# A two-layer three-branch decoder trunk: gating constants made early, row scaling on ScalarE, one more pair of columns as seven products, and a shorter last sum of squares

## The chip, the cores and the metric

One core of a Trainium2 chip runs the whole computation in one launch. Its engines are named as in the profile: PE (TensorE, matrix products into PSUM), DVE (VectorE), ACT (ScalarE), POOL (GpSimd) and SP (SyncE, which here only issues DMAs). The metric is the device time of one execution in microseconds (us). Most executions of a kernel agree within 0.3%.

## The reference, cut to what matters

Each of two layers normalizes x (512 tokens, 1024 channels, float32), projects it on 8704 columns, mixes tokens in three branches and adds a gated, projected merge to x. A last RMSNorm follows.

```
def hybrid_layer(x, ...):
    h = rmsnorm(x, norm_g)
    aq, ak, av, az, buv, bz, cq, ck, cv, cz, gl = split_cols(h @ w_in)
    # A: differential attention, then RMSNorm over each head's 128 outputs
    oa = rmsnorm(diff_attention(qa, ka, va, lam), subln_g) * (1 - lam_init)
    ya = oa * silu(az)
    # B: causal spatial gating in chunks of 128 tokens
    u, vb = split(gelu(buv));  vb = layernorm(vb, sgu_ln_g, sgu_ln_b)
    w_causal = sgu_w * tril(ones(128, 128))
    mixed = einsum('gts,bnsgc->bntgc', w_causal, vb) + sgu_b
    yb = u * mixed * silu(bz)
    # C: three dilated window attentions, mixed by their softmax sums
    yc = oc * silu(cz)
    pb = [ya @ w_branch[0], yb @ w_branch[1], yc @ w_branch[2]]
    merged = sum(sigmoid(gl[n]) * pb[n] for n in range(3))
    return x + merged @ w_out
out = rmsnorm(layer_2(layer_1(x)), final_g)
```

## The kernel before, in words

The state is kept transposed, channels on partitions and tokens in the free dimension. Every projection is done in float32 by three products of rounded parts (`mm3`, L408 to 411: high by high, low by high, high by low). A weight half of 128x512 numbers, a slot, is rounded by ScalarE into its high part (L170), and the remainder is the low part (L171), on VectorE or, for every fifth slot after the first 32, on POOL (`LOMOD`, `FIRST_G`). Two raw buffers of 512 KB are filled from SP's queue (`load`), and up to six slots are made ahead (`NSLOT`).

A pair of 128-column blocks is projected in one of two ways. Those listed in `EIGHT` take 24 products of 512 columns for each block (`proj_T`, L417). All others take seven products of quarters in place of eight (`seven`, L503), with 256 columns in each product: seven slots (L176 to 203) of which four are made from sums of raw quarters by POOL, VectorE, POOL, POOL (L192 to 195), and combinations of the products by ScalarE (L531, L535), VectorE and POOL (`add`, L528). The sums of quarters lie in tiles of the tag `pr`, two buffers, which attention's probabilities use too (L862).

`plan` (L50) lists the items of a layer in order. First come the gating values `vb`, the values of A (with the normalized x made beside them), the values of C (with the mixed quarters made beside them, `mix`, L596) and one pair. Then attention A runs over four heads in three steps each, and the remaining pairs are pulled in as fill between its products; the two second-gate pairs `bz2` (columns of bz, multiplied into u by POOL at L653) are the second last projection in attention A and the last in attention C. Attention C follows in the same way, and then the gating step `sgu`, in turn with the sigmoid gates `gl2` and the branch projections `pb`, and last the output projection `out`.

`i_sgu` (L657) loads the bias row and the 128x512 matrix for the layer from ScalarE's queue, after the newest weight instructions (`behind_weights`), lets POOL clear the upper triangle (L666), sums the matrix over its partitions by a product with ones (L671) and makes `add` from it, bias and the layernorm's shift, four VectorE instructions on 128x128 (L675). After that it does four groups: four products (L685), two VectorE instructions (L690, L695), one split.

In attention A, after a head's third step, VectorE multiplies the head's 128x512 outputs in PSUM by four row factors (`scaled`, L943; the factors come from POOL at L941), and `finish` transposes the result and applies the gate. In the last layer the output blocks 4 to 7 are done for the left 256 tokens and then for the right 256; `square` (L278) sums squares over blocks, `rms_sum` (L380) sums over partitions by small products with ones, and `final` (L824) normalizes and stores.

Each engine works through its own list in order. The lists are written by a planner that takes the program's order and priorities and its own simulated times, so an edit can move instructions that it does not touch.

Of the kernel before, what the change touches and what calls it, by code (L numbers as in the profile page):

```python
# [10 lines left out]
F32 = mybir.dt.float32  # L11
# [32 lines left out]


EIGHT = {("pp", br, i) for br in (BR_A, BR_C) for i in range(6) if (br, i) != (BR_C, 5)}
EIGHT |= {("bz2", 0), ("bz2", 2), ("gl2", BR_B, 0)}


def plan():  # L50
# [50 lines left out]
def hybrid_kernel(ctx: ExitStack, tc, xT, posr, wpack, tabs, cvec, pvec, rvec, lamv, sguw, outT):  # L101
# [149 lines left out]
    class X:  # L251


        def __init__(self, first=False):
            self.first = first
            self.h = att.tile([P, KC, S], F32R, tag="vs", name="xuh")
            self.l = []
            self.f = []
            self.ss = t2k("ob", name="ssum")

        def raw(self, kc):
            if kc % 2 == 0:
# [15 lines left out]
        def square(self, kc, c=slice(0, S), part=False):  # L278
            xf = self.f[kc // 2][:, kc % 2, c]
            if kc == 0:  # L280
                A.activation(out=self.ss[:, c], in_=xf, func=AF.Square)
            else:
                sq = t2k("t1", name="sq")
                A.activation(out=sq[:, c], in_=xf, func=AF.Square)
                if part and kc == KC - 1:
                    self.sq = sq
                    return
                (V if kc == KC - 1 or self.first or c.start else G).tensor_tensor(out=self.ss[:, c], in0=self.ss[:, c], in1=sq[:, c], op=ALU.add)

# [90 lines left out]
    def rms_sum(sqs):  # L380

        n = sqs[0].shape[-1] // P
        ps = ps_s()[:, 0, :]
        for b in range(n):
            for i, sq in enumerate(sqs):
                T.matmul(
                    ps[:, b : b + 1], lhsT=sq[:, b * P : (b + 1) * P], rhs=ones[:, 0:1], start=i == 0,
                    stop=i == len(sqs) - 1,
                )
        ro = sm.tile([P, 4], F32, tag="ro", name="ro")[:, :n]  # L390
        V.tensor_scalar(out=ro, in0=ps[:, :n], scalar1=1.0 / D, scalar2=EPS, op0=ALU.mult, op1=ALU.add)
        rp = sm.tile([P, 4], F32, tag="rp", bufs=2, name="rp")[:, :n]
        G.tensor_tensor(out=rp, in0=ro, in1=mhalf[:, :n], op=ALU.pow)
        return rp
# [153 lines left out]
    def layer(l, xu, parts):  # L548
# [47 lines left out]
        def mix(kc):  # L596
            with behind_weights():
                if kc == 0:
                    split_x(KC - 1)
                    norm["mix"] = mixes(xu.f)  # L600
                next(norm["mix"])
                if kc == KC - 1:
                    next(norm["mix"])
                    if l == 0:
                        lambdas()

        def pair(it, use, bank=ps_pj):

# [47 lines left out]

        def i_sgu():  # L657
            vb, uz = sgu["vb"], sgu["uz"]
            sgw = [att.tile([P, S], F32, tag="kl", bufs=2, name="sgw") for _ in range(2)]
            with behind_weights():  # L660
                nc.scalar.dma_start(out=sgw[0], in_=rvec[l : l + 1, :].partition_broadcast(P))
                nc.scalar.dma_start(out=sgw[1], in_=sguw[l])
            t = att.tile([P, 2, 4, S], F32R, tag="vs", name="yB")
            yhl[BR_B] = [[t[:, 0, 0:2], t[:, 0, 2:4]], [t[:, 1, 0:2], t[:, 1, 2:4]]]
            wc = sgw[1].rearrange("p (g t) -> p g t", g=4)
            G.affine_select(  # L666
                out=wc, in_=wc, pattern=[[0, 4], [1, P]], base=0, channel_multiplier=-1, compare_op=ALU.is_ge,
                fill=0.0,
            )
            pw = ps_s()[:, 0, :]  # L670
            T.matmul(pw, lhsT=ones, rhs=sgw[1], start=True, stop=True)  # L671
            add = t2k("t1", name="add")
            for g in range(4):
                gs = slice(g * P, (g + 1) * P)
                V.scalar_tensor_tensor(  # L675
                    out=add[:, gs], in0=pw[:, gs], scalar=ln[:, l, 1, g : g + 1], in1=sgw[0][:, gs], op0=ALU.mult,
                    op1=ALU.add,
                )
            yield 0.9
            for g in range(4):  # L680
                if g % 2 == 0:
                    pms = ps_s()
                pm = pms[:, g % 2, :]
                for tb in range(4):
                    T.matmul(  # L685
                        pm[:, tb * P : (tb + 1) * P], lhsT=vb[:, tb, g * P : (g + 1) * P],
                        rhs=wc[:, g, :], start=True, stop=True,
                    )
                ob = t2k("ob")
                V.scalar_tensor_tensor(  # L690
                    out=ob.rearrange("p (n t) -> p n t", n=4), in0=pm.rearrange("p (n t) -> p n t", n=4),
                    scalar=ln[:, l, 0, g : g + 1],
                    in1=add[:, g * P : (g + 1) * P].unsqueeze(1).to_broadcast([P, 4, P]), op0=ALU.mult, op1=ALU.add,
                )
                V.scalar_tensor_tensor(  # L695
                    out=ob, in0=ob, scalar=0.25, in1=uz[g // 2][:, g % 2, :], op0=ALU.mult, op1=ALU.mult
                )
                split(yhl[BR_B][0][g // 2][:, g % 2, :], yhl[BR_B][1][g // 2][:, g % 2, :], ob)
                yield 0.9

        def i_val(br):
            if br == BR_A:
# [12 lines left out]
            for tb in range(4):  # L715
                p8 = banks[tb].rearrange("p (h e) -> p h e", h=8)
                r, o = norm["rst"][:, tb : tb + 1], v[:, tb]
                A.activation(out=o[:, :, 0:64], in_=p8, func=AF.Copy, scale=r)
                V.scalar_tensor_tensor(
                    out=o[:, :, 64:128], in0=p8, scalar=r, in1=o[:, :, 0:64].bitcast(F32), op0=ALU.mult,  # L720
                    op1=ALU.subtract,
                )

        def i_pp(br, i):
            def use(n, ps, own):
# [97 lines left out]

        def final(c):  # L824
            x_ = xn[0]
            bc = rms_spread(rms_sum([x_.ss[:, c], x_.sq[:, c]]))
            for e in range(KC):
                xf = x_.f[e // 2][:, e % 2, c]
                V.scalar_tensor_tensor(out=xf, in0=xf, scalar=fg[:, e : e + 1], in1=bc, op0=ALU.mult, op1=ALU.mult)
                (nc.sync, nc.scalar)[e % 2].dma_start(out=outT[e, :, c], in_=xf)  # L830
# [70 lines left out]
        def attention_a(fill):  # L901
# [4 lines left out]
            for n in range(13):  # L906
# [10 lines left out]
                if prev is not None:  # L917
# [20 lines left out]
                    if 3 in prs:  # L938
# [3 lines left out]

                        def scaled(po_=po_, r0_=so_):  # L943
                            on = t2k("ob", name="on").rearrange("p (i e) -> p i e", i=4)
                            V.tensor_tensor(
                                out=on, in0=po_, in1=r0_.unsqueeze(2).to_broadcast([P, 4, P]), op=ALU.mult
                            )
                            return on

                        def finish(h=h):  # L950
# [197 lines left out]
```

## Time and profile before

| | |
|---|---|
| median of 3 executions | 1116.62 us (1115.82 to 1116.85) |
| the profiled execution | 1117.34 us, span 1115.6 us |
| PE busy | 1087.3 us, 97% of the span |
| DVE busy | 823.6 us, 74% |
| ACT busy | 598.9 us, 54% |
| POOL busy | 471.4 us, 42% |
| HBM read | 100.58 MB, 94 GB/s with what is written |

The span is what the profiler saw between the first and the last instruction. Products on PE are pipelined, and their ends are modelled; the distance of two starts is what one of them takes of PE's time. An idle engine only costs where something on the way to the end waits for it.

### The profile page before, as it was taken

To read this page: it belongs to the slowest core of one execution; us is meant where nothing else is said; L and a number is where in the kernel's file an instruction comes from. 1 tells how busy PE (TensorE), PEld (TensorE's weight loads), DVE (VectorE), ACT (ScalarE), POOL (GpSimd) and SP (SyncE) were. 2 spreads that over 40 slices of the span, in tenths; PEclk is the share of its full clock that TensorE was granted. 3 is DMA by queue.
4 is the path that set the end of the run, shared out by engine and by line. 5 is a ranking of instruction groups with operands and counts; after the bars stand their busy time and mean duration, and the time that the engine had idled before them with its cause. 6 is when DMAs were issued, how large, how long until landed. Compare 5 with 4: busy or idle time off the path is not lost.

```text
span 1115.6 us, 17803 instructions
## 1 busy us (share of the span) xinstructions
PE 1087.3 (97%) x6444; PEld 939.6 (84%) x6444; DVE 823.6 (74%) x1519; ACT 598.9 (54%) x1281; POOL 471.4 (42%) x419
## 2 busy tenths in 40 slices
PE   8999999999999999999999999999999999999996
PEld 6787878878778999998888888887888889999886
DVE  6678869877969877774436779787788877787544
ACT  6554747486774444453435456565778534444430
POOL 4004443434534676644211343534342536667420
PEclk9999999999999999999999999999999999999998
DMA  5431313220312233244523313122111313333433
GB/s 194 135 103 58 95 58 96 95 76 1 114 58 87 87 112 102 92 148 152 188 83 103 98 38 114 57 76 76 58 58 57 112 59 101 107 97 103 142 110 99
DMA packets 35064, 105.97 MB, mean 95 GB/s; under 512 B 4704, under 2 KB 7776, under 8 KB 34976
## 3 DMA queue, kind: packets, MB, share of 16 engines
q1 hardware_dynamic: 29936, 98.50, 27.6%
q10 hardware_dynamic: 5040, 6.34, 1.8%
q8 instruction: 51, 0.84, 0.3%
q14 instruction: 37, 0.30, 0.1%
HBM read 100.58 MB, written 4.24 MB: 94 GB/s over the span
## 4 chain that ended last, share of the span: by engine, by line
PE 85%; DVE 5%; DMA 3%; issue 2%; ACT 2%; POOL 1%; POOLq 0%; DVEq 0%; SPq 0%; ACTq 0%
PE ps_pj L409 15%; PE ps_pj L411 14%; PE ps_pj L410 14%; PE ps_to L409 8%; PE ps_to L411 8%; PE ps_to L410 8%; PE ps_s L858 3%; DMA raw<-in_wpack 2%; PE ps_to L898 2%; PE ps_to L434 2%; PE ps_to L436 2%; PE ps_to L435 2%; DVE wlo L171 1%; PE ps_to L929 1%; PE ps_to L1004 1%
## 5 line engine op out<-in xcount | busy, mean ns | idle before, releaser
L170 ACT ACTIVATE whi<-raw 128x512 fp32r<-128x512 f32 x316 | 195.0, 627 | 246.3 <-DMA raw<-in_wpack 74.2
L171 DVE TENSOR_TENSOR wlo<-raw,whi 128x512 fp32r<-128x512 f32 x261 | 223.0, 862 | 99.2 <-ACT whi L170 91.1
L409 PE MATMUL ps_pj<-xh,whi 128*128 128x512 f32 (+1 forms) x544 | 207.9, 382 | 1.0 <-DVE z L462 1.0
L411 PE MATMUL ps_pj<-xh,wlo 128*128 128x512 f32 (+1 forms) x544 | 204.5, 376 | 0.0
L410 PE MATMUL ps_pj<-xl,whi 128*128 128x512 f32 (+1 forms) x544 | 204.0, 375 | 0.0
L171 POOL TENSOR_TENSOR wlo<-raw,whi 128x512 fp32r<-128x512 f32 x55 | 78.8, 1433 | 169.6 <-ACT whi L170 158.2
L409 PEld LDWEIGHTS ps_pj<-xh,whi 128*128 128x128 f32 x544 | 102.6, 189 | 20.0 <-issue 1.6
L411 PEld LDWEIGHTS ps_pj<-xh,wlo 128*128 128x128 f32 x544 | 102.5, 188 | 18.2 <-issue 0.9
L410 PEld LDWEIGHTS ps_pj<-xl,whi 128*128 128x128 f32 x544 | 102.7, 189 | 17.6 <-issue 1.8
L452 POOL TENSOR_TENSOR rsh<-rsh,sinr 128x512 f32<-128x512 f32 x32 | 42.3, 1322 | 132.8 <-DVE rsh L450 121.3
L171 DVE TENSOR_TENSOR wlo<-t,whi 128x512 fp32r<-128x512 f32 x88 | 81.2, 940 | 16.2 <-ACT whi L170 16.0
L411 PE MATMUL ps_to<-mh,wlo 128*128 128x256 f32 x320 | 90.5, 284 | 0.5 <-DVE wlo L171 0.4
L409 PE MATMUL ps_to<-mh,whi 128*128 128x256 f32 x320 | 90.8, 284 | 0.2 <-ACT ea L531 0.2
L410 PE MATMUL ps_to<-ml,whi 128*128 128x256 f32 x320 | 90.4, 283 | 0.0
L874 ACT ACTIVATE pr<-pr,nm 128x128 f32<-128x128 f32 (+3 forms) x128 | 70.6, 553 | 36.4 <-DVE nm L870 36.1
L170 ACT ACTIVATE whi<-t 128x512 fp32r<-128x512 f32 x112 | 65.8, 624 | 42.0 <-DVE t L193 23.4
L409 PE MATMUL ps_to<-xh,whi 128*128 128x256 f32 x240 | 68.5, 285 | 2.6 <-DVE zs L528 2.5
L411 PE MATMUL ps_to<-xh,wlo 128*128 128x256 f32 x240 | 68.4, 286 | 0.7 <-DVE wlo L171 0.7
L410 PE MATMUL ps_to<-xl,whi 128*128 128x256 f32 x240 | 68.2, 284 | 0.0
L870 DVE CUSTOM_DVE_ANT_0 pr<-ps_s,tab 128x128 f32<-128x128 f32 (+3 forms) x128 | 56.2, 483 | 11.8 <-PE ps_s L858 8.3
L409 PEld LDWEIGHTS ps_to<-mh,whi 128*128 128x128 f32 x320 | 61.4, 192 | 1.0 <-ACT ea L531 0.4
L411 PEld LDWEIGHTS ps_to<-mh,wlo 128*128 128x128 f32 x320 | 61.3, 192 | 1.2 <-DVE wlo L171 0.9
(238 smaller groups left out, 2844.9 us busy)
## 6 DMA issues: line engine op xcount, KB each, us to landing
raw<-in_wpack SPq DMA_DIRECT2D x174, 512.0 KB
xf<-in_xT SPq DMA_DIRECT2D x8, 256.0 KB
xr<-in_xT ACTq DMA_DIRECT2D x8, 256.0 KB
x1d<-xf SPq DMA_DIRECT2D x8, 256.0 KB
raw<-in_wpack SPq DMA_DIRECT2D x4, 256.0 KB
xr<-x1d ACTq DMA_DIRECT2D x4, 256.0 KB
xr<-x1d ACTq DMA_DIRECT2D x8, 128.0 KB
out<-xf SPq DMA_DIRECT2D x8, 128.0 KB
```

Of the source, the lines that this page charges most:

```text
L170: newest[0] = A.activation(out=hi, in_=src, func=AF.Copy).ins
L171: r = (G if on_g else V).tensor_tensor(out=lo, in0=src, in1=hi.bitcast(F32), op=ALU.subtract)
L409: T.matmul(ps, lhsT=wh, rhs=mh, start=first, stop=False)
L410: T.matmul(ps, lhsT=wh, rhs=ml, start=False, stop=False)
L411: T.matmul(ps, lhsT=wl, rhs=mh, start=False, stop=last)
L434: T.matmul(banks[tb], lhsT=mh_[:, ts], rhs=wh, start=kc == 0, stop=False)
L435: T.matmul(banks[tb], lhsT=ml_[:, ts], rhs=wh, start=False, stop=False)
L436: T.matmul(banks[tb], lhsT=mh_[:, ts], rhs=wl, start=False, stop=kc == KC - 1)
L452: G.tensor_tensor(out=sh, in0=sh, in1=sinr, op=ALU.mult)
L858: T.matmul(pss[:, m, at[i]], lhsT=q[HALF[m], a, qs], rhs=k[HALF[m], b, :W], start=t == 0, stop=t == 2,)
L870: V.tensor_tensor_reduce(out=o, in0=pss[:, m, at[i]], in1=tab[:, 0 if br == BR_A else 1, S - W :], op0=ALU.add, op1=ALU.min, scale=-0.125, ...
L874: A.activation(out=o, in_=o, func=AF.Exp, scale=-1.0, bias=nm[:, m : m + 1], accum_out=den[:, m : m + 1],)
```

## The change

Four edits, in both layers unless said otherwise.

1. The pair `("bz2", 0)` leaves `EIGHT` and is so projected by seven products.
2. The gating step's transfers and mask move to a function `gating`, called while the values of branch C are projected (after the third of eight blocks in `mix`); the product with ones and the four constant instructions move to `gating_add`, called at the end of that projection. The constants are written over the bias row, so that a tile of the tag `t1` is no longer used.
3. `scaled` uses four ScalarE instructions on 128x128, each with a factor per row, in place of one on VectorE.
4. At the end, the squares of the last two blocks (before: of the last) are not added up but passed to `rms_sum`, which sums three tiles for each 128 tokens. For the halves of 256 tokens the small products go tile by tile, the two sums lie in two PSUM banks, and the scale and epsilon are applied by one instruction for each.

```diff
-EIGHT |= {("bz2", 0), ("bz2", 2), ("gl2", BR_B, 0)}
+EIGHT |= {("bz2", 2), ("gl2", BR_B, 0)}
...
-                if part and kc == KC - 1:
-                    self.sq = sq
+                if part and kc >= KC - 2:
+                    self.sq[kc] = sq
                     return
...
+        ps2 = ps_s()
+        todo = [(b, i) for b in range(n) for i in range(len(sqs))]
+        if n == 2:
+            todo.sort(key=lambda t: t[1])
+        sums = [ps2[:, b % 2 if n == 2 else 0, b : b + 1] for b in range(n)]
+        for b, i in todo:
+            T.matmul(
+                sums[b], lhsT=sqs[i][:, b * P : (b + 1) * P], rhs=ones[:, 0:1], start=i == 0, stop=i == len(sqs) - 1
+            )
         ro = sm.tile([P, 4], F32, tag="ro", name="ro")[:, :n]
-        V.tensor_scalar(out=ro, in0=ps[:, :n], scalar1=1.0 / D, scalar2=EPS, op0=ALU.mult, op1=ALU.add)
+        for o, p in [(ro, ps2[:, 0, :n])] if n == 4 else [(ro[:, b : b + 1], sums[b]) for b in range(n)]:
+            V.tensor_scalar(out=o, in0=p, scalar1=1.0 / D, scalar2=EPS, op0=ALU.mult, op1=ALU.add)
...
+                if kc == 2:
+                    gating()
...
+        def gating():
+
+            sgu["w"] = add, wc = [att.tile([P, S], F32, tag="kl", bufs=2, name="sgw") for _ in range(2)]
+            with behind_weights():
+                nc.scalar.dma_start(out=add, in_=rvec[l : l + 1, :].partition_broadcast(P))
+                nc.scalar.dma_start(out=wc, in_=sguw[l])
+            w4 = wc.rearrange("p (g t) -> p g t", g=4)
+            G.affine_select(
+                out=w4, in_=w4, pattern=[[0, 4], [1, P]], base=0, channel_multiplier=-1, compare_op=ALU.is_ge,
+                fill=0.0,
+            )
+
+        def gating_add():
+            add, wc = sgu["w"]
+            pw = ps_s()[:, 0, :]
+            T.matmul(pw, lhsT=ones, rhs=wc, start=True, stop=True)
+            for g in range(4):
+                gs = slice(g * P, (g + 1) * P)
+                V.scalar_tensor_tensor(
+                    out=add[:, gs], in0=pw[:, gs], scalar=ln[:, l, 1, g : g + 1], in1=add[:, gs], op0=ALU.mult,
+                    op1=ALU.add,
+                )
...
+            gating_add()
...
-            bc = rms_spread(rms_sum([x_.ss[:, c], x_.sq[:, c]]))
+            bc = rms_spread(rms_sum([x_.ss[:, c], x_.sq[KC - 2][:, c], x_.sq[KC - 1][:, c]]))
...
-                            V.tensor_tensor(
-                                out=on, in0=po_, in1=r0_.unsqueeze(2).to_broadcast([P, 4, P]), op=ALU.mult
-                            )
+                            for i in range(4):
+                                A.activation(out=on[:, i, :], in_=po_[:, i, :], func=AF.Copy, scale=r0_[:, i : i + 1])
```

## Rows read from the trace of the kernel before

**Rows 1.** Busy us of each engine in stretches of 20 us, granted clock, DMA.
```profile
180.00:200.00 20.00, 20.00 (x113) 16.69 (x110) 19.26 (x38) 14.68 (x36) 6.05 (x8) 1.00 0.26 80
...
320.00:340.00 20.00, 16.79 (x125) 14.85 (x124) 17.03 (x26) 11.73 (x22) 10.60 (x10) 1.00 0.33 107
340.00:360.00 20.00, 19.48 (x140) 17.71 (x140) 19.24 (x29) 9.57 (x17) 10.89 (x8) 1.00 0.27 79
...
700.00:720.00 20.00, 19.01 (x110) 15.94 (x109) 14.59 (x28) 10.82 (x28) 13.12 (x9) 1.00 0.16 53
...
820.00:840.00 20.00, 17.53 (x120) 15.39 (x120) 19.89 (x40) 14.07 (x31) 11.79 (x17) 1.00 0.34 107
...
880.00:900.00 20.00, 19.20 (x140) 17.34 (x139) 19.20 (x34) 9.89 (x18) 8.54 (x6) 1.00 0.35 106
900.00:920.00 20.00, 17.46 (x101) 15.52 (x100) 12.74 (x18) 7.94 (x15) 9.77 (x8) 0.91 0.17 54
```

**Rows 2.** PE's waits: releaser, us in total, times, longest.
```profile
PE ps_to L409 <- DVE zs L528: 2.5, 1, 2.5
...
PE ps_s L685 <- DVE add L675: 1.3, 1, 1.3
...
PE ps_s L671 <- POOL sgw L666: 0.5, 1, 0.5
```

**Rows 3.** Timelines of DVE and POOL, 320 to 345: start, duration, [idle before].
```profile
335.56 1.11 DVE L675 SCALAR_TENSOR_TENSOR add<-ps_s,pv,sgw 128x128 f32<-128x128 f32 x4
...
332.40 1.00 POOL L666 TENSOR_SCALAR_AFFINE_SELECT sgw<-sgw 128x512 f32<-128x512 f32 x1 [4.22 <-DMA sgw<-in_sguw]
```

**Rows 4.** The chain of waits, 865 to 912, in order: start, us.
```profile
872.94 5.00 DMA raw<-in_wpack
...
880.63 3.42 DMA raw<-in_wpack
```

**Rows 5.** Timeline of PE, at 50 and at 384: start, modelled duration.
```profile
49.62 0.39 PE L434 MATMUL ps_s<-whi,xuh 128*128 128x512 f32 x1
...
50.30 0.39 PE L434 MATMUL ps_s<-whi,xuh 128*128 128x512 f32 x1
...
383.98 0.28 PE L409 MATMUL ps_to<-mh,whi 128*128 128x256 f32 x1
...
384.34 0.28 PE L409 MATMUL ps_to<-mh,whi 128*128 128x256 f32 x1
```

**Rows 6.** Groups by line and shape: count | busy us, mean ns | idle before.
```profile
L171 DVE TENSOR_TENSOR wlo<-t,whi 128x512 fp32r<-128x512 f32 x88 | 81.2, 940 | 16.2 <-ACT whi L170 16.0
...
L170 ACT ACTIVATE whi<-t 128x512 fp32r<-128x512 f32 x112 | 65.8, 624 | 42.0 <-DVE t L193 23.4 <-PE ps_to L411 4.7 <-POOL t L194 4.1
...
L192 POOL TENSOR_TENSOR t<-raw 128x512 f32<-128x512 f32 x28 | 36.8, 1313 | 43.3 <-DMA raw<-in_wpack 25.6 <-PE ps_to L898 6.9 <-ACT ea L531 5.5
...
L528 DVE TENSOR_TENSOR eb<-ps_to,ea 128x256 f32<-128x256 f32 x40 | 16.5, 415 | 4.4 <-PE ps_to L411 4.0
...
L892 ACT ACTIVATE pr<-pr,rd 128x128 f32<-128x128 f32 x16 | 5.4, 388 | 0.0
...
L945 DVE TENSOR_TENSOR on<-ps_to,so 128x512 f32<-128x512 f32 x8 | 5.4, 679 | 0.3 <-POOL so L941 0.3
```

**Rows 7.** Timelines of DVE and POOL, 225 to 262.
```profile
232.56 1.44 DVE L171 TENSOR_TENSOR wlo<-raw,whi 128x512 fp32r<-128x512 f32 x1
...
236.83 0.69 DVE L171 TENSOR_TENSOR wlo<-raw,whi 128x512 fp32r<-128x512 f32 x1 [0.60 <-ACT whi L170]
...
232.16 1.28 POOL L452 TENSOR_TENSOR rsh<-rsh,sinr 128x512 f32<-128x512 f32 x1 [1.84 <-DVE rsh L450]
```

**Rows 8.** Timelines of PE and ACT at the end.
```profile
1106.24 0.36 PE L386 MATMUL ps_s<-ones,ssum 128*128 128x1 f32 x2
1106.47 0.36 PE L386 MATMUL ps_s<-ones,sq 128*128 128x1 f32 x2
...
1105.48 0.42 ACT L284 ACTIVATE sq<-xf 128x256 f32<-128x256 f32 x1 [0.59 <-DVE xf L813]
```

More of the change, by code (lines that the diff above doesn't have):

```diff
@@ L259, in __init__ @@
             self.ss = t2k("ob", name="ssum")
+            self.sq = {}
         def raw(self, kc):
@@ L382, in rms_sum @@
         n = sqs[0].shape[-1] // P
[L383 to L388, printed above, removed]
-                )
+        ps2 = ps_s()
[7 more added lines that the diff above has]
+            )
         ro = sm.tile([P, 4], F32, tag="ro", name="ro")[:, :n]
-        V.tensor_scalar(out=ro, in0=ps[:, :n], scalar1=1.0 / D, scalar2=EPS, op0=ALU.mult, op1=ALU.add)
+        for o, p in [(ro, ps2[:, 0, :n])] if n == 4 else [(ro[:, b : b + 1], sums[b]) for b in range(n)]:
+            V.tensor_scalar(out=o, in0=p, scalar1=1.0 / D, scalar2=EPS, op0=ALU.mult, op1=ALU.add)
         rp = sm.tile([P, 4], F32, tag="rp", bufs=2, name="rp")[:, :n]
@@ L658, in i_sgu @@
             vb, uz = sgu["vb"], sgu["uz"]
[L659 to L662, printed above, removed]
             t = att.tile([P, 2, 4, S], F32R, tag="vs", name="yB")
             yhl[BR_B] = [[t[:, 0, 0:2], t[:, 0, 2:4]], [t[:, 1, 0:2], t[:, 1, 2:4]]]
[L665 to L679, printed above, removed]
+            add, wc = sgu["w"]
             for g in range(4):
@@ L686, in i_sgu @@
                         pm[:, tb * P : (tb + 1) * P], lhsT=vb[:, tb, g * P : (g + 1) * P],
-                        rhs=wc[:, g, :], start=True, stop=True,
+                        rhs=wc[:, g * P : (g + 1) * P], start=True, stop=True,
                     )
@@ L699, in i_sgu @@
                 yield 0.9
+        def gating():
[9 more added lines that the diff above has]
+        def gating_add():
+            add, wc = sgu["w"]
+            pw = ps_s()[:, 0, :]
[6 more added lines that the diff above has]
+                )
         def i_val(br):
@@ L944, in scaled @@
                             on = t2k("ob", name="on").rearrange("p (i e) -> p i e", i=4)
-                            V.tensor_tensor(
-                                out=on, in0=po_, in1=r0_.unsqueeze(2).to_broadcast([P, 4, P]), op=ALU.mult
-                            )
+                            for i in range(4):
+                                A.activation(out=on[:, i, :], in_=po_[:, i, :], func=AF.Copy, scale=r0_[:, i : i + 1])
                             return on
```

## The prediction

> **What bounds the kernel now.** I read the stretches of 20 us first, then TensorE's waits, then the order of time around those waits. TensorE is the bound: through attention A it shows 20.00 us busy of 20, as in 180 to 200, although VectorE is nearly full there (19.26) and ScalarE is not (14.68) [rows 1]. So work taken off TensorE counts in full as long as its operands come in time, and work taken off another engine counts only where TensorE waits for it. It waits in few places. In layer 0 it is busy for 16.79 us in 320 to 340 and 19.48 in 340 to 360; in layer 1 for 17.53 in 820 to 840, 19.20 in 880 to 900 and 17.46 in 900 to 920 [rows 1]. The two waits that carry the lines of the gating branch are both in layer 0: 0.5 us for the masked matrix (`sgw`, POOL) and 1.3 for the constants (`add`, VectorE); the largest of layer 1 is 2.5 us for a combination of the seven products (`zs`) [rows 2]. In order of time, layer 0 shows why: POOL sits idle 4.22 us until the matrix has landed, masks it in 1.00, and VectorE makes the constants in 1.11, late in a stretch in which it is also wanted for weights [rows 3]. Layer 1 has the same steps with no wait right at them, but the weight load that starts beside the two gating transfers takes 5.00 us, the one after it 3.42, and the chain runs through weights and VectorE to the 2.5 us wait [rows 2, 4].
>
> **The gating constants, moved ahead.** Both transfers, the mask, the product with ones and the four constant instructions leave the gating step; nothing of them is dropped, and the four later steps of the branch stay. At the old place layer 0 loses the two waits: 0.5 + 1.3 = 1.8 us [rows 2]. What is late next is VectorE, 17.03 busy in 320 to 340 and 19.24 in 340 to 360, from which the 1.11 us of constants go too [rows 1, 3]. The gain has the ends 0, if TensorE meets VectorE's queue 1.8 us earlier and waits there, and 3.7, all of TensorE's idle time from 320 to 360 [rows 1]; I take 1.8, because as much work as is needed to keep pace goes from VectorE as well. In layer 1 VectorE has 19.20 us of 20 in 880 to 900 and the wait of 2.5 us lies behind it; four constants as in layer 0 are 1.1 us less ahead of it [rows 1, 2, 3]. The 1.6 us between 5.00 and 3.42 run at the same time and I don't add them [rows 4]. Ends: 0, and 2.5 plus what the clock costs (below); I take 1.1.
>
> At the new place the steps must be paid for. The transfers are issued on ScalarE's queue while the values of branch C are projected, two weight slots of 512 columns per 12 matmuls each, so a weight load is wanted every 24 x 0.227 = 5.4 us [rows 5] and takes 3.4 to 5.0 [rows 4]; six slots ahead (16 us) cover that, and without the cover TensorE would wait 1.6 us once per layer. The mask now waits on POOL's queue; behind it can stand only a weight remainder that is wanted slots later, so the 4.22 us cost nothing unless that slot is next, when they cost at most that much. The product with ones keeps its TensorE time. VectorE's 1.1 us come before attention A, with a whole projection (10.9 us, below) until the scores want the same PSUM tile. I count zero.
>
> **The pair as seven products.** Now it is two projections of 24 matmuls of 512 columns; spacing (50.30 - 49.62)/3 = 0.227 us, so 48 x 0.227 = 10.9. Seven products of 12 matmuls of 256 columns at (384.34 - 383.98)/3 = 0.120 are 84 x 0.120 = 10.1 [rows 5]. That is 0.8 us per layer, and not an eighth of the pair, because half the columns take more than half the time.
>
> The price lies on the other engines. Seven weight slots in place of four: three more remainders at 0.94 = 2.8 on VectorE; one sum of quarters with POOL's work beside it, at 1.44; six combinations at 0.41 = 2.5: together 6.7 us per layer [rows 6, 7]. ScalarE gets three roundings at 0.62 and two evictions of half the columns, between 0.39 and 0.62, so some 2.9 us; POOL three sums or differences, at 1.31, and one of half the columns, which I put at 1.0: 4.9 [rows 6]. The pair runs at 185 to 201 in layer 0, in the stretch with 0.74 us of VectorE free [rows 1]. Two more things go with it. The sums of quarters live in the two buffers that attention's probabilities use, so POOL has to wait until attention gives them up, and attention until the slots are made. And slots are counted, every fifth remainder going to POOL; three more per layer shift which ones for all that follows, with either sign. What a seven-product pair costs inside attention is to be seen at those already there: nothing where the last products of the pair of `u2` run (180 to 200), 0.99 us around the other one of layer 1 (700 to 720), 2.47 around the pair in attention C (820 to 840) [rows 1]. I take 0.5, between the two in attention A, since the pair lies there. Net: 2 x (0.8 - 0.5) = 0.6 us gained; ends 1.6 gained and 2 x (2.47 - 0.8) = 3.3 lost.
>
> A row shows one more price. A remainder took 0.69 us on VectorE alone and 1.44 where POOL's rope product, started 0.4 us earlier, ran beside it [rows 7]. The Trainium skill (SBUF — State Buffer, "Who interferes with whom") says that a VectorE instruction with two SBUF inputs and a GpSimd one that reads SBUF exclude each other, the second waiting for the first to end. The trace agrees in kind: 1.44 is 0.75 more, under the 1.28 of the POOL instruction. By that rule the pair's POOL work would come on top of its VectorE work as a whole, and it is the second rival below.
>
> **The scaling on ScalarE.** Per head one VectorE instruction (0.68) goes and four on 128x128 of 0.39 come, at most 1.6 us on ScalarE; 8 heads, so 5.4 us leave VectorE and up to 12.4 arrive [rows 6]. ScalarE has 5.3 us in 20 free in the fullest stretch of attention A [rows 1]. Behind them in its queue stand exponentials and weight roundings, which now wait if the row factors from POOL are late; TensorE waits for those. Ends: 1.0 gained (the wait in 700 to 720, where VectorE was late) and 8 x (1.6 - 0.7) = 7 lost if each head's step were on the path. I take 0, as TensorE runs without a gap there and its next use of the scaled tile is a later, queued step.
>
> **The final sum of squares.** One add goes; its square is summed on TensorE instead. Behind the last square (ends 1105.48 + 0.42 = 1105.90) four pairs of small matmuls stand today, the last starting at 1106.47, 0.23 after the one before [rows 8]; two remain behind it, ending about 1105.95 + 2 x 0.23 + 0.1 = 1106.5 against 1106.83 (1106.47 + 0.36): 0.3 gained. In the left half two more pairs stand in TensorE's unbroken row: 2 x 0.23 = 0.5 lost. Two small scale instructions for one overlap with the pairs. I count 0, ends 0.3 gained and 0.5 lost.
>
> **The sum.** 1.8 + 1.1 + 0.6 = 3.5 us. The profiled execution took 1117.34 us (span 1115.6), 0.72 above the median 1116.62; 1117.34 - 3.5 = 1113.8, on the median's level 1113.1.
>
> **Rivals.** *The waits only move.* TensorE arrives earlier at weights that VectorE has not made. For it: 19.24 and 19.20 of 20 [rows 1]. Against: 1.1 us of VectorE's own work goes from each place. Then the gating brings 0.5 in all, the pair 0.6: 1115.5. A planner orders each engine's instructions anew from its simulated times, and if it puts the moved steps elsewhere, this is the time too.
>
> *The pair starves TensorE.* VectorE gets 6.7 us, and 4.9 from POOL's sums if these shut it out, less two scalings (1.4): 10.2 in a stretch with 0.7 to 4 us free [rows 1, 6, 7]. From 1.5 + 0.8 = 2.3 us of TensorE waiting per pair the change gains nothing, from 3.4 it is slower by more than 0.2%. At 5.5, a little over half of that load, 2 x (5.5 - 0.8) - 2.9 = 6.5 lost on the median: 1123; at 4.0 it is 1120. For it: 2.47 lost at the pair in attention C [rows 1]; against: the pairs of `u2` cost 0 to 1. I put it at 1120.5.
>
> *Layer 1 gains its whole wait.* The granted clock is 0.91 in 900 to 920, which is 20 x 0.09 x 2 = 3.6 us at 1.2 in place of 2.4 GHz, 1.8 us lost, behind a wait of 2.5 [rows 1, 2]. If 1.1 us less VectorE work and the quicker load take away the wait and the fall of the clock, layer 1 gives 4.3 instead of 1.1: 1109.9.
>
> **How the numbers follow.** Forecast (1111 to 1114.4) 0.48; waits only move 0.26; pair starves 0.16; whole wait 0.10. What this kernel's measurement can tell from no change is about 0.2%, 2.2 us. Faster: 0.48 + 0.10 = 0.58; within: 0.26; slower: 0.16. The range goes from 1109.0, under the third rival, to 1118.5, over the first and into the second until about 0.12 is left above; the forecast's own range is 1111 to 1114.4.
>
> **What would show it.** The two waits of [rows 2] on L671 and L685 are gone, with the mask near 65 and 600 us; TensorE is over 18.5 busy in 320 to 340. The seven products of the pair end 0.8 us sooner, with no wait over 1 us between 180 and 205 or 725 and 745; VectorE full there with TensorE under 19 would prove the second rival. A wait in 340 to 360 or 890 to 910 as long as before proves the first. It is wrong if the pair costs more than 2.3 us of waiting, or ScalarE's exponentials come late in attention A.

## The result: 9.7 us slower, and the profile after

The changed kernel takes 1126.47 us (median of 4 executions, 1125.51 to 1128.00) against 1116.73 for the kernel before (1115.82 to 1118.82): a ratio of 1.0086, interval 1.0068 to 1.0104. That is slower by 9.7 us, above the predicted range. The profiled execution took 1126.75 us, its span is 1125.0. One execution of 4197.66 us and one of the kernel before of 1714.81 us, both among the experiments below, were in a slow state and are left out of the medians and ratios given.

The 20-us stretches of the changed kernel that answer to [rows 1] come first (columns as there); what lay at 700 to 720, 820 to 840 and 880 to 920 is later by 8 to 16 us.

```profile
180.00:200.00 20.00, 15.03 (x115) 13.95 (x114) 18.71 (x40) 14.71 (x43) 9.54 (x11) 0.89 0.28 79
200.00:220.00 20.00, 20.00 (x115) 17.92 (x115) 18.88 (x30) 10.19 (x21) 9.22 (x9) 0.94 0.22 74
320.00:340.00 20.00, 20.00 (x145) 18.22 (x144) 11.63 (x24) 13.78 (x30) 5.95 (x8) 1.00 0.16 54
340.00:360.00 20.00, 17.53 (x129) 16.02 (x128) 19.94 (x30) 10.59 (x20) 9.25 (x6) 1.00 0.26 79
740.00:760.00 20.00, 14.39 (x96) 13.67 (x95) 16.84 (x36) 13.07 (x34) 6.03 (x8) 0.83 0.33 106
840.00:860.00 20.00, 17.29 (x104) 14.58 (x103) 19.97 (x37) 15.85 (x33) 11.61 (x13) 1.00 0.42 124
900.00:920.00 20.00, 19.05 (x126) 17.09 (x125) 18.91 (x28) 10.42 (x20) 9.01 (x7) 1.00 0.24 80
```

The loss is where the pair is projected. TensorE was busy for all of 180 to 200 before and is now for 15.03 us of it, at a granted clock of 0.89; in layer 1 it is busy for 14.39 of 740 to 760, at 0.83. TensorE's waits (columns of [rows 2]) name the steps that came late.

```profile
PE ps_pj L413 <- DVE zs L532: 6.7, 2, 4.5
...
PE ps_s L870 <- DVE nm L882: 4.6, 3, 2.7
PE ps_pj L415 <- DVE wlo L171: 2.4, 3, 1.1
PE ps_s L673 <- DVE ob L678: 1.8, 2, 0.9
```

The two waits of the gating branch in [rows 2] are gone. New at the top are the combinations of the seven products (`zs`) and the first VectorE step on a block of scores (`nm`). Both lie around the pair, and TensorE's order of time in layer 0 shows them: start, modelled duration, [idle before and its releaser].

```profile
186.72 0.28 PE L413 MATMUL ps_pj<-xh,whi 128*128 128x256 f32 x1
186.84 0.28 PE L414 MATMUL ps_pj<-xl,whi 128*128 128x256 f32 x1
...
194.25 0.96 PE L870 MATMUL ps_s<-k,q 64*128 64x512 f32 x6 [2.74 <-DVE nm L882]
197.44 0.58 PE L413 MATMUL ps_pj<-mh,whi 128*128 128x256 f32 x1 [2.23 <-DVE zs L532]
...
198.03 0.42 PE L415 MATMUL ps_pj<-mh,wlo 128*128 128x256 f32 x1
198.25 0.41 PE L413 MATMUL ps_pj<-mh,whi 128*128 128x256 f32 x1
...
743.86 0.96 PE L870 MATMUL ps_s<-k,q 64*128 64x512 f32 x6 [1.16 <-DVE nm L882]
749.27 0.58 PE L413 MATMUL ps_pj<-mh,whi 128*128 128x256 f32 x1 [4.45 <-DVE zs L532]
```

A product of 256 columns follows the one before it by 0.12 us ahead of the two waits and by 0.22 behind them. The 5-us stretches give the clock in between:

```profile
190.00:195.00 5.00, 2.26 (x19) 1.80 (x18) 5.00 (x10) 5.00 (x14) 2.16 (x5) 1.00 0.60 197
195.00:200.00 5.00, 2.77 (x14) 2.56 (x13) 5.00 (x12) 3.39 (x10) 0.30 (x1) 0.55 0.38 100
200.00:205.00 5.00, 5.00 (x37) 5.00 (x36) 4.68 (x11) 2.79 (x6) 1.27 (x1) 0.77 0.02 7
```

A mean of 0.55 over 5 us is 4.5 us at the lower level, 1.2 GHz in place of 2.4 (2 x 0.45 x 5), and 0.77 is 2.3 us more: 6.8 us together, behind 5 us in which TensorE stood still for 2.74. From 197.44 on, 4.9 of them were worked through at half speed, which loses 2.4 us. So layer 0 loses 2.74 + 2.23 + 2.4 and gains the 0.8 of the pair: 6.6. In layer 1 the clock is low for 2 x 0.17 x 20 = 6.8 us again:

```profile
745.00:750.00 5.00, 0.73 (x3) 0.73 (x4) 5.00 (x14) 3.83 (x13) 0.00 (x0) 0.84 0.28 84
750.00:755.00 5.00, 5.00 (x26) 5.00 (x25) 2.79 (x8) 1.04 (x2) 0.00 (x0) 0.50 0.05 20
```

A mean of 0.84 up to 750 puts the fall at 748.4 (2 x 0.16 x 5 = 1.6 us before), so some 6.0 of the 6.8 lie behind 749.27: 1.16 + 4.45 + 3.0 - 0.8 = 7.8. Measured from the first score product of attention A to the first of attention C, attention A takes 130.7 and 132.0 us; in the same kernel with the pair put back (first experiment) it takes 124.3 and 124.1. The differences, 6.4 and 7.9, agree with these sums.

What VectorE did in the meantime, in layer 0 of the changed kernel:

```profile
187.56 3.27 DVE L475 SCALAR_TENSOR_TENSOR gw<-gw,zs 128x512 f32<-128x512 f32 x2 [0.90 <-ACT gw L474]
190.75 0.68 DVE L477 SCALAR_TENSOR_TENSOR uz<-gth,zs 128x512 f32<-128x512 f32 x1
191.36 1.28 DVE L171 TENSOR_TENSOR wlo<-t,whi 128x512 fp32r<-128x512 f32 x2
192.56 0.68 DVE L475 SCALAR_TENSOR_TENSOR gw<-gw,vb 128x512 f32<-128x512 f32 x1
193.16 0.55 DVE L882 CUSTOM_DVE_ANT_0 pr<-ps_s,tab 128x384 f32<-128x384 f32 x1
...
194.12 1.73 DVE L171 TENSOR_TENSOR wlo<-t,whi 128x512 fp32r<-128x512 f32 x1
195.77 0.68 DVE L477 SCALAR_TENSOR_TENSOR uz<-gth,zs 128x512 f32<-128x512 f32 x1
196.37 0.68 DVE L171 TENSOR_TENSOR wlo<-raw,whi 128x512 fp32r<-128x512 f32 x1
196.97 0.41 DVE L532 TENSOR_TENSOR zs<-ps_pj,ea 128x256 f32<-128x256 f32 x1
```

It does not rest between 187.56 and 202.5. The scores that TensorE needs taken up stand behind two GELU steps of the pair before (`gw`, 3.27 us), one more (`uz`), the pair's remainders and a GELU step of the gating values (`gw<-gw,vb`); the combination that it waits for next stands behind a remainder of 1.73 us, another `uz` and another remainder. Attention's own work and the gating values' GELU were there before; the pair put its steps between them. Beside the two `gw`, POOL makes the pair's last sums (1.30 and 1.75 us from 187.28 on), and the two `gw` take 3.27 us where they take 1.29 with those sums gone (run with POOL's sums on ScalarE, below).

### The profile page after: what moved, and what is told of

Read it like the earlier page. It is cut to its first block, busy times and chain, and to the rows that moved or that the text cites. A ratio compares the mean times of both kernels' runs of the same rounds, so it can differ in the third digit from the quotient of the medians.

```text
span 1125.0 us, 18041 instructions
## 1 busy us (share of the span) xinstructions
PE 1089.3 (97%) x6524; PEld 947.8 (84%) x6524; DVE 840.0 (75%) x1531; ACT 611.8 (54%) x1323; POOL 484.4 (43%) x427
## 4 chain that ended last, share of the span: by engine, by line
PE 84%; DVE 7%; DMA 3%; issue 2%; ACT 2%; POOL 1%; SPq 0%; POOLq 0%; DVEq 0%; ACTq 0%
PE ps_pj L413 14%; PE ps_pj L415 14%; PE ps_pj L414 14%; PE ps_to L413 8%; PE ps_to L415 8%; PE ps_to L414 8%; PE ps_s L870 3%; PE ps_to L910 2%; DMA raw<-in_wpack 2%; DVE wlo L171 2%; PE ps_to L438 2%; PE ps_to L440 2%; PE ps_to L439 2%; PE ps_to L1015 1%; PE ps_to L941 1%
## 5 line engine op out<-in xcount | busy, mean ns | idle before, releaser
L171 DVE TENSOR_TENSOR wlo<-raw,whi 128x512 fp32r<-128x512 f32 x258 | 226.4, 883 | 94.6 <-ACT whi L170 83.8
L413 PE MATMUL ps_pj<-xh,whi 128*128 128x512 f32 (+1 forms) x536 | 202.1, 377 | 0.5 <-DVE z L466 0.5
L415 PE MATMUL ps_pj<-xh,wlo 128*128 128x512 f32 (+1 forms) x536 | 198.9, 371 | 0.0
L414 PE MATMUL ps_pj<-xl,whi 128*128 128x512 f32 (+1 forms) x536 | 198.4, 370 | 0.0
L415 PEld LDWEIGHTS ps_pj<-xh,wlo 128*128 128x128 f32 x536 | 101.0, 188 | 16.6 <-issue 0.9
L171 DVE TENSOR_TENSOR wlo<-t,whi 128x512 fp32r<-128x512 f32 x96 | 88.1, 937 | 15.6 <-ACT whi L170 15.3
L170 ACT ACTIVATE whi<-t 128x512 fp32r<-128x512 f32 x120 | 70.4, 624 | 47.8 <-DVE t L193 27.6
L414 PEld LDWEIGHTS ps_to<-ml,whi 128*128 128x128 f32 x320 | 61.4, 192 | 0.1
```

Source lines behind the costliest of these rows:

```text
L170: newest[0] = A.activation(out=hi, in_=src, func=AF.Copy).ins
L171: r = (G if on_g else V).tensor_tensor(out=lo, in0=src, in1=hi.bitcast(F32), op=ALU.subtract)
L413: T.matmul(ps, lhsT=wh, rhs=mh, start=first, stop=False)
L414: T.matmul(ps, lhsT=wh, rhs=ml, start=False, stop=False)
L415: T.matmul(ps, lhsT=wl, rhs=mh, start=False, stop=last)
```

## The experiments

All were timed in six rounds beside the kernel before, which stood at 1116.9 to 1117.4 us; each ratio is to it, with its interval in parentheses. The expectations number five theories. The pair loses the time, since VectorE has more to do at its place than there is time for (1); the buffers that the pair's sums share with attention's probabilities hold it (2); the scaling on ScalarE delays evictions and exponentials (3); a seven-product pair costs so much anywhere in attention A (4); shared buffers and scaling each hold the chain up alone, so that both must go (5). Two more have no number: POOL's sums shut VectorE out, and the place in the order costs, whoever scales.

**The pair put back.** In the changed kernel the pair is projected by 48 products again.

```diff
-EIGHT |= {("bz2", 2), ("gl2", BR_B, 0)}
+EIGHT |= {("bz2", 0), ("bz2", 2), ("gl2", BR_B, 0)}
```

> The changed kernel with one part undone: the pair bz2 0 is projected by 48 products of 512 columns again; the early gating constants, the scaling on ScalarE and the new last sum stay. Theory 1 (VectorE's load at the pair's place) and theory 2 (the sums of quarters take both buffers of attention's probabilities, so that scores and sums wait for each other) both say that the pair alone made the kernel slower: by the offsets of the stages, attention A then loses nothing, the product with ones costs 2 x 1.6 us early, and the gating step gives back 2.5 us in layer 0 and 6 in layer 1: 1116.7 + 3.2 - 8.5 = 1111, within 1109.5 to 1113.5. Theory 3 (the scaling on ScalarE holds up the exponentials) says that most of the loss stays: 1120 or more.

Measured: 1109.85 us, ratio 0.9934 (0.9921 to 0.9948), as theories 1 and 2 had it and not 3. The pair costs 16.6 us, and the three other edits gain about 7. No version that computes everything is faster; the pair-free ones below, 1110.36 to 1110.58, are level with it. Its stretch where the changed kernel stood still is full again, with VectorE nearly as busy as in [rows 1]:

```profile
180.00:200.00 20.00, 20.00 (x119) 16.85 (x118) 18.70 (x39) 15.80 (x43) 7.05 (x9) 1.00 0.30 97
```

**The pair alone.** The kernel before, with the pair as its only edit (the diff above, the other way round).

> The kernel before with one part of the change alone: the pair bz2 0 as seven products. Theories 1 and 2: attention A loses 6 to 8 us in each layer, as in the changed kernel: 1116.7 + 2 x 7 = 1130, within 1126 to 1133. Theory 1 expects the upper half, as the scaling is on VectorE too (0.7 to 1.4 us more at the place). Theory 3: the pair alone gains its 0.8 us per layer or costs little: 1114 to 1119.

Measured: 1132.82 us, ratio 1.0144 (1.0131 to 1.0158), 15.7 us lost, within the range of theories 1 and 2. With the other edits or without, the pair costs 16 us. Here TensorE waits 7.8 us in all for `nm` and 3.4 for `zs`.

**The gating constants alone.** The changed kernel with pair, scaling and last sum as before.

> The kernel before with the early gating constants alone (pair, scaling and last sum as before). By the stages of the changed kernel with the pair back, nearly all of its gain lies in the two gating steps: 1116.9 less 6 to 7, that is 1110 to 1111. If the scaling on ScalarE carries part of it, this one stays at 1112 to 1114.

Measured: 1110.40 us, ratio 0.9942 (0.9930 to 0.9955), as expected. The move of the constants is worth 6.5 us by itself, practically the whole gain of the pair-free version. The stretch that showed a clock of 0.91 in [rows 1] is at full clock here:

```profile
900.00:920.00 20.00, 20.00 (x128) 18.20 (x127) 16.03 (x22) 8.94 (x17) 15.52 (x11) 1.00 0.30 94
```

**The scaling, with and without the pair.** The same edit to the changed kernel and to the version with the pair put back:

```diff
-for i in range(4):
-    A.activation(out=on[:, i, :], in_=po_[:, i, :], func=AF.Copy, scale=r0_[:, i : i + 1])
+V.tensor_tensor(out=on, in0=po_, in1=r0_.unsqueeze(2).to_broadcast([P, 4, P]), op=ALU.mult)
```

> The changed kernel with the scaling of a head's outputs back on VectorE, one instruction in place of four on ScalarE. Theory 1: VectorE gets 0.7 to 1.4 us more at the place where TensorE waits for it, in each layer: 1127 to 1130. Theory 2: the same time, 1125 to 1128. Theory 3: faster by several us, 1116 to 1121.

> The changed kernel with the pair as 48 products and the scaling back on VectorE: what is left is the early constants and the new last sum. The scaling off the path of TensorE: the same as with it on ScalarE, 1109 to 1111. If VectorE's relief by 0.7 us per head matters without the pair as well: 1112 or more.

Measured: 1126.11 (ratio 1.0091, 1.0074 to 1.0107) and 1110.36 (0.9942, 0.9930 to 0.9955). Neither differs from its twin, 1126.47 and 1109.85, by more than the intervals: the scaling's engine is worth nothing that can be told in either kernel. Theory 3 falls as an account of the changed kernel as it stands. Theory 1 had put 0.7 to 1.4 us more per layer on VectorE at 1127 to 1130, theory 2 at 1125 to 1128; the interval does not part these. But the pair alone, with the scaling on VectorE, costs no more (15.7) than with it on ScalarE (16.6).

**Buffers of its own.** The pair's sums of quarters leave the tag that attention's probabilities use; below, with the scaling back on VectorE as well.

```diff
-t12, t34 = t4k("pr", 2, name="t12"), t4k("pr", 2, name="t34")
+t12, t34 = (t4k(*(("ptl", 3) if g[1] == C_BZ else ("pr", 2)), name=w) for w in ("t12", "t34"))
```

> The changed kernel, but the sums of quarters of the pair bz2 0 alone lie in two buffers of the tag ptl, which nothing uses during attention A, in place of the two buffers of attention's probabilities. The instructions and their number are the same. Theory 2: attention's scores no longer wait for the pair's slots nor the sums for attention; the waits of 5 us per layer and the fall of the clock behind them go: 1111 to 1115. Theory 1: VectorE's load is unchanged; at most 1 us per layer is won: 1124 to 1127.

> The changed kernel with the pair's sums of quarters in two buffers of their own (tag ptl) and the scaling back on VectorE, both at once. Each alone moved little. Theory 1: VectorE's load stays what limits: 1123 to 1127. Theory 5 (each of the two holds the chain up alone, the shared buffers by the scores, the scaling by ScalarE's queue, which waits for the row factors from POOL): both must go together, then most of the loss goes: 1111 to 1117.

Measured: 1125.03 (1.0076, 1.0063 to 1.0088) and 1122.35 (1.0041, 1.0027 to 1.0055). The first is in theory 1's range, the second just under it and far from theory 5's 1111 to 1117. The buffers alone give 1.4 us, within the intervals. In the first run the clock no longer falls at the pair in either layer, but TensorE's waits spread over other steps:

```profile
PE ps_to L910 <- DVE pr L897: 4.0, 3, 2.2
PE ps_pj L413 <- ACT ea L535: 3.0, 2, 1.7
PE ps_s L870 <- DVE nm L882: 2.6, 3, 1.5
```

So theory 2 is at most a small part as long as VectorE's load stays. With the buffers apart, the scaling does matter, by 2.7 us. The buffers are not wholly the pair's own: attention C's first tiles have the tag `ptl` too, and POOL waits 2.95 us for a remainder of the pair before it clears one at 194.38.

**Less load on VectorE.** The two VectorE instructions in each GELU of the gating values are left out (part of the computation); the second run does the same with the pair put back, as a control.

```diff
-gelu2(o, o)
+A.activation(out=o, in_=o, func=AF.Square), A.activation(out=o, in_=o, func=AF.Tanh, scale=0.044715 * GELU_C)
```

> The changed kernel with work left out: the GELU of the gating values vb loses its two VectorE instructions for each block of 128 tokens (the tanh of the square goes straight into the tile), some 2.2 us of VectorE for each of four blocks per layer, two of which lie at the pair's place. To be read against the same kernel with the pair as 48 products. Theory 1: VectorE's overrun at the place falls by 2 to 4 us per layer, so the difference of the two falls from 16.6 us to 8 to 12, this one being at 1115 to 1121. Theory 4: the difference stays above 14.

> The control for the kernel with less GELU work: the same two VectorE instructions of the gating values' GELU are left out, and the pair bz2 0 is projected by 48 products of 512 columns. TensorE doesn't wait for VectorE at this place, so all theories expect little from the work left out: 1107 to 1110, against 1109.9 with the GELU whole.

Measured: 1113.58 (0.9969, 0.9954 to 0.9984) and 1107.14 (0.9906, 0.9893 to 0.9919). With these steps the pair costs 16.6 us, without them 6.4: 10.2 of the 16.6 hang on VectorE's load, more than theory 1 expected (4.6 to 8.6), and theory 4's 14 is out. The stretch of the first run:

```profile
180.00:200.00 20.00, 18.01 (x147) 16.76 (x146) 18.67 (x46) 14.83 (x43) 9.87 (x12) 1.00 0.25 73
```

VectorE is as busy as in the changed kernel (18.71), but has done 46 instructions there in place of 40, and TensorE, busy for 18.01 instead of 15.03, keeps its full clock. A busy share that stays the same does not show that the load stayed.

**POOL's sums on ScalarE.** The three sums that POOL makes for the pair become ScalarE copies of one of the two operands (part of the computation).

```diff
+if g[1] == C_BZ and e is G: A.activation(out=o, in_=i0, func=AF.Copy)
+else: e.tensor_tensor(out=o, in0=i0, in1=i1, op=op)
```

> The changed kernel; POOL's three sums of quarters for the pair bz2 0 are replaced by copies of their first quarter on ScalarE (work left out: the pair's weights are then not the right ones), so that 4 us per layer of POOL work with two SBUF inputs go, and VectorE's instructions stay as they are. If POOL's sums stretch VectorE's instructions beside them: 1126.5 less 2 to 8 us, 1118 to 1124. If VectorE's own 6.7 us per layer are the whole cause: 1125 to 1128.

Measured: 1129.18 us, ratio 1.0110 (1.0096 to 1.0124), above both sums; a gain would have borne out that POOL's sums shut VectorE out, and there is none. VectorE has its time back: the two `gw` take 1.29 us together, not 3.27, and of 180 to 200 it works 16.60 us. TensorE works no more than in the changed kernel. Its stretch at the pair,

```profile
180.00:200.00 20.00, 14.00 (x107) 12.80 (x106) 16.60 (x40) 15.70 (x43) 4.32 (x8) 0.92 0.28 80
```

and TensorE's waits:

```profile
PE ps_to L910 <- DVE pr L897: 4.7, 1, 4.7
PE ps_pj L413 <- ACT zs L539: 3.7, 1, 3.7
PE ps_pj L413 <- ACT ea L535: 3.6, 2, 2.3
```

It waits for probabilities and for ScalarE's evictions now. The edit loads ScalarE with what it takes from POOL, so it does not price the stretched instructions. It does show that a VectorE with gaps isn't enough here.

**The pair later.** Its turn comes two items later in attention A, behind the GELU of one more block of gating values (`vbg`) and branch C's first pair (q and k of head 0, 48 products).

```diff
-a += [("u2", 2), ("vbg", 0), ("bz2", 0), ("vbg", 1), ("pp", BR_C, 0), ("vbg", 2)]
+a += [("u2", 2), ("vbg", 0), ("pp", BR_C, 0), ("vbg", 1), ("bz2", 0), ("vbg", 2)]
```

> The changed kernel with one swap in the order of a layer: the pair bz2 0 comes after the pair pp C 0 (48 products of 512 columns), so that two seven-product pairs (u2 2 and bz2 0) no longer follow each other with the GELU of u2 and of the gating values between them. Theory 1 (VectorE has more to do at that place than there is time): its work is spread over 11 us more, TensorE's waits fall from 5.5 to 8 us per layer to 0 to 2: 1109 to 1114. Theory 4 (a seven-product pair costs so much anywhere in attention A, since the scores there can't wait): still 1122 or more.

Measured: 1119.58 us, ratio 1.0014 (1.0006 to 1.0023), between the sums of theories 1 and 4, so both missed. 6.9 us come back; 9.7 are still lost against the kernel without the pair. Three more runs take from those 9.7, each with an edit already shown: less GELU (part of the computation left out), buffers of its own, and these with the scaling on VectorE.

> The changed kernel with the pair after pp C 0 and with less GELU work (the gating values' GELU without its two VectorE instructions, as in the control with the pair back, 1107.1). Theory 1: with the work spread and 2.2 us less of VectorE per block there is room, and the pair at last pays its 0.8 us per layer or breaks even: 1105 to 1108.5. If shared buffers hold up the scores whatever VectorE has to do: 1111 to 1115.

> The changed kernel with the pair after pp C 0 and its sums of quarters in two buffers of their own. Without them it took 1119.6. Shared buffers as the rest of the loss: 1110 to 1113. VectorE's load as the rest: 1117 to 1120.

> The changed kernel with the pair after pp C 0, own buffers for its sums, and the scaling of the heads back on VectorE. Without the last edit 1113.3. If ScalarE's queue is what is left of the loss: 1109 to 1111, level with the kernel without the pair (1109.9). If VectorE's load is: 1113 to 1116.

Measured: 1117.50 (1.0003, 0.9992 to 1.0015), 1113.30 (0.9970, 0.9958 to 0.9982) and 1114.29 (0.9974, 0.9961 to 0.9987). At the later place theory 1 missed: without the GELU steps only 2.1 us come back, in a run that spreads from 1115.2 to 1120.5 and fits neither sum. VectorE sits idle there and then works through three remainders ahead of the scores:

```profile
198.80 0.69 DVE L419 TENSOR_TENSOR q<-t,q 128x512 fp32r<-128x512 f32 x1 [3.78 <-ACT q L418]
...
201.47 4.38 DVE L171 TENSOR_TENSOR wlo<-t,whi 128x512 fp32r<-128x512 f32 x3
205.77 0.68 DVE L882 CUSTOM_DVE_ANT_0 pr<-ps_s,tab 128x512 f32<-128x512 f32 x1
```

There the shared buffers hold 6.3 of the 9.7, and the scaling adds nothing that can be told, as the sum for VectorE's load had it. The best of these is still 3.5 us behind the kernel without the pair.

**Both holders removed at the first place.** Own buffers and less GELU (part of the computation left out), then these with the scaling on VectorE.

> The changed kernel at the pair's first place, with less GELU work and with two buffers of their own for its sums of quarters. With less GELU work alone it is 6.4 us behind its control (1113.6 against 1107.1). If the shared buffers are the rest: 1106.5 to 1109. If something else is (ScalarE's queue with the scaling, or VectorE's own load from the pair): 1111 to 1114.

> The changed kernel with the pair's sums in buffers of their own, the row scaling back on VectorE, and the two VectorE instructions of the gating values' GELU left out (work left out: the GELU is not the reference's). The same without the scaling's return took 1117.4. If what was left there is ScalarE's queue (a scaling that waits for POOL's row factors with an eviction behind it), the scaling's return takes that away: 1108 to 1111, and TensorE's waits on the evictions at the pair (3.0 us, twice) go. If the place itself costs, whoever scales: 1115 to 1119.

Measured: 1117.42 (1.0001, 0.9990 to 1.0011) and 1112.03 (0.9955, 0.9941 to 0.9968). The first missed both sums: it is slower than less GELU alone (1113.58). ScalarE's order of time in it shows what stands ahead of an eviction that TensorE waits for:

```profile
192.97 1.14 ACT L958 ACTIVATE on<-ps_to,so 128x128 f32<-128x128 f32 x4 [1.48 <-POOL so L953]
193.99 0.64 ACT L476 ACTIVATE gth<-gw 128x512 f32<-128x512 f32 x1
194.51 0.64 ACT L170 ACTIVATE whi<-t 128x512 fp32r<-128x512 f32 x1
195.03 0.39 ACT L535 ACTIVATE ea<-ps_pj 128x256 f32<-128x256 f32 x1
```

ScalarE stands for 1.48 us until POOL has the row factors and scales for 1.14; a GELU step, a rounding and the eviction (`ea`) that TensorE waits 1.7 us for stand behind. With less GELU alone, ScalarE doesn't stand still ahead of the scaling, and the clock in 180 to 200 is 1.00; here it falls:

```profile
180.00:200.00 20.00, 16.74 (x125) 15.45 (x124) 16.88 (x45) 14.38 (x42) 9.46 (x11) 0.92 0.17 54
```

With the scaling on VectorE, 5.4 us come back, between the two sums that were expected and nearer to that of ScalarE's queue, and the wait for `ea` is gone. In this last run VectorE, the shared buffers and ScalarE's queue are all relieved, and against the control without the pair (1107.14) the pair still costs 4.9 us; of those 1.8 and 2.0 lie in the two attentions A (126.1 us each against 124.3 and 124.1). In what is left there,

```profile
PE ps_s L870 <- DVE nm L882: 2.0, 2, 1.3
PE ps_pj L413 <- DVE zs L532: 1.7, 3, 1.0
```

the combinations and scores are still late on VectorE, by little each. The pair's own steps on VectorE are still all there, so these 4.9 us are theirs and the place's together; no run parts the two.

**Another pair with 48 products.** In the version with the pair put back, branch C's last pair (k and z of head 3), which takes seven products, is projected by 48 too.

```diff
-EIGHT = {("pp", br, i) for br in (BR_A, BR_C) for i in range(6) if (br, i) != (BR_C, 5)}
+EIGHT = {("pp", br, i) for br in (BR_A, BR_C) for i in range(6)}
```

> The changed kernel with two pairs as 48 products: bz2 0, and the last pair of attention C, which was seven products before too. Theory 1 (seven products cost more than 0.8 us of TensorE's time wherever VectorE is full) : TensorE's waits in attention C, 0.6 us in layer 0 and 2.8 in layer 1 with bz2 0 back, go for 2 x 0.8: 1107 to 1109.5 against 1109.9. If the waits there belong to attention C itself: 1111 to 1112.

Measured: 1110.58 us, ratio 0.9941 (0.9928 to 0.9955), between the two sums: no gain over 1109.85. The 0.8 us of TensorE's time per layer that seven products save there don't show in the time. Nor do the waits that 48 products were to take away: layer 1 has a wait that the version with the pair put back doesn't have,

```profile
927.05 0.58 PE L413 MATMUL ps_to<-mh,whi 128*128 128x256 f32 x1 [2.54 <-ACT ea L535]
```

with the clock at 0.67 in 925 to 930.

## Why the prediction was wrong

**The pair: the failed step.** "I take 0.5" of waiting per pair, taken from the pairs of `u2`, gave a gain of 0.6 us. It cost 16.6. TensorE's own price was right: its products stand 0.12 us apart up to the wait, as in [rows 5]. The waiting was 5.0 us in layer 0 and 5.6 in layer 1, with 2.4 and 3.0 more at the lower clock, not 0.5. The 0.99 us from which the 0.5 came (700 to 720 in the kernel before) was not even a wait for the combinations of seven products: a product of the pair waited there until VectorE had made a gate (`z`, L462) of a block before it.

```profile
717.17 0.38 PE L409 MATMUL ps_pj<-xh,whi 128*128 128x256 f32 x1 [0.99 <-DVE z L462]
```

The pairs of `u2` come behind pairs with 48 products. This one comes behind one of them, with that one's GELU steps and those of a gating value still on VectorE, in a stretch that [rows 1] showed at 19.26 of 20. The prediction had this row and the load, 6.7 us of VectorE work on 0.74 free, and still took the wait from a neighbour. The load should have been set against the free time: 6.7 less 1.4 for two scalings less 0.74 free is 4.6 us too much, and with the 3.0 by which two `gw` and a remainder are stretched beside POOL (3.27 - 1.29 + 1.73 - 0.68) it is 7.6; TensorE waited 5.0 and 5.6. That count would have warned, but it is no price: the scaling's 1.4 us, put back on VectorE, showed no loss (1126.11 against 1126.47).

**The rival that came true.** The pair starved TensorE, beyond the 5.5 us of its larger sum: 7.4 and 8.6 us per pair, the clock included. Its condition (TensorE under 19 with VectorE full) stood, 15.03 with 18.71. Left out of it was the clock, which fell during the second of the two waits. By its second half, POOL's sums come on top of VectorE's work. The Trainium skill (SBUF — State Buffer, "Who interferes with whom") has a VectorE instruction with two SBUF inputs and a POOL one that reads SBUF wait for each other; the two `gw`, 3.27 us beside those sums and 1.29 without them, agree in kind. That it sets the loss is not borne out: without those sums nothing came back, though ScalarE then carried three copies.

**The gating constants: right in kind, 3.6 us too small.** 2.9 us were forecast, 6.5 were measured alone. Both waits went, and mask and constants are done by 68 and 80 us in layer 0, far ahead. From the start of the last score product of attention C to that of the last branch projection, the constants alone shorten layer 0 by 2.7 us (199.3 to 196.6; 1.8 forecast) and layer 1 by 5.8 (201.5 to 195.7; 1.1 forecast); some 1.4 are given back elsewhere. Layer 1 is what the third rival described: the wait of 2.5 us is gone, and no fall of the clock is left in 900 to 920, 1.00 in place of 0.91 [rows 1]. The term of 1.1 us, four instructions' time, was mis-sized: they stood ahead of a wait, and with it went the slow clock behind it, 4.3 of the 5.8 us by that rival's sum. The other 1.5 were not followed.

**The scaling: zero, as forecast,** by two pairs of runs. The condition that was named (factors from POOL late, exponentials and roundings behind) does occur, once the buffers are apart: then it costs 2.7 and 5.4 us at the pair's first place.

**The end: as forecast.** From the last output product to the end of the span, 10.98 us became 10.65, 0.3 gained; in the left half, the two further pairs of small products, four starts 0.11 us apart, take 0.4. The sum is nothing.

**What stays open.** The profiled spans with the pair and with it put back differ by 16.2 us, of which 14.3 are accounted for by the waits and the clock in attention A. 2.0 more lie in attention C of layer 0 and 1.1 between layer 0's last branch projection and attention A of layer 1, with 1.2 less elsewhere; no run took these apart. Of the 16.6 us by the medians, the runs put 10.2 down to VectorE's load (the GELU steps left out, with the buffers shared); how the other 6.4 divide among buffers, ScalarE's queue and the place is open, since these don't add up. Nor is it settled why POOL's sums, moved away, gave nothing: they went to ScalarE, and a run that drops them without loading another engine wasn't made. And the planner orders every engine's list anew for each edit, so a difference of a few us between two runs can be the new order's as well as the edit's; no run held the order fixed.

## What to carry to other kernels

When work is taken from the bounding engine and given to the others, set the added load of each against its free time in that very stretch, not against its mean over the span (75% here) and not against what the same trick cost at another place. Where the queue is already full, expect waits of the size of the overrun (here 4.6 us by the count, 5.0 and 5.6 measured), and the slow clock behind them, which took half as much again. Holders do not add up: relieving one (the buffers 1.4 us, the scaling 0, POOL 0) may show nothing as long as another holds, and the same edit is worth 6.3 us (the buffers) at another place or 5.4 (the scaling) with the others relieved.

## What the runs showed of the hardware that was not expected

- TensorE's granted clock fell from 2.4 to 1.2 GHz for 6.8 us in each layer, each time during the second of two waits at the pair (2.74 and 2.23 us; 1.16 and 4.45). Shorter waits did not settle it: with own buffers for the pair (1.7 us at most on the evictions, 2.2 on the probabilities) the clock stayed at 1.00 there, and with own buffers and less GELU (1.5 and 1.7 us) it was at 0.92 in 180 to 200, which is 3.2 us at the lower level.
- A fall of the clock that isn't at the change can be the change's: early constants took away the one at 900 to 920.
- VectorE instructions on 128x512 with two SBUF inputs took longer where POOL's ran beside them: a remainder 1.73 us in place of 0.68, and two `gw` 3.27 us together, 1.29 with POOL's sums gone.
